# Attention scores on three PSUM banks, broadcasts and small transposes on the two banks of the attention transposes

## The chip, the cores and the metric

The kernel runs on one core of a Trainium2 chip. The metric is the device time of one execution in microseconds. The engines are called as the profile calls them: PE (TensorE, the matrix engine; PEld is its weight load), DVE (VectorE), ACT (ScalarE), POOL (GpSimd), SP (SyncE, which issues the DMAs). Matmuls write to PSUM, which has eight banks of 512 float32 values in each of 128 partitions; this kernel uses all eight.

## The reference, cut to what matters

Two layers over 1024 latent tokens and 256 context tokens, width 1024. Each layer is a mixer of three head groups on one input projection, and a gated MLP with a convolution of width 3:

```python
h = modulate(rms_norm(x, norm1_g[i]), sh1, sc1)
a_z, bq, bk, bv, cq, ck, cv = split_proj(h @ w_in[i])
out_a = chunk_gmlp(a_z, a_ws[i], a_bs[i])                               # A: gMLP over chunks of 128
out_b = window_attn_latent(q_b, k_b, v_b, k_bc, v_bc, b_sink[i])        # B: 8 heads, window +-128, context
s = jnp.einsum('bqhmd,bkhmd->bhmqk', q, k).astype(jnp.float32) * q.shape[-1] ** -0.5
p = jax.nn.softmax(s, axis=-1)                                          # C: 4 heads, two maps each,
pd = p[:, :, 0] - lam * p[:, :, 1]                                      #    all 1280 keys
o_c = jnp.einsum('bhqk,bkhd->bqhd', pd.astype(v.dtype), v)
x = x + g1 * (jnp.concatenate([out_a, out_b, out_c], axis=-1) @ w_out[i])
x = x + g2 * conv_ffn(modulate(rms_norm(x, norm2_g[i]), sh2, sc2),
                      w_up[i], conv_w[i], conv_b[i], w_down[i])         # d_ff 2816
```

The context tokens go through the same layer (not in the last one), and attend to context tokens alone.

## The kernel before, in words

The code is written straight down, and a scheduler of the build then orders each engine's instructions: an instruction that stands later in the text goes ahead of an earlier one if its inputs and its buffer are there sooner. Tiles come from pools; each name (tag) in a pool has so many buffers, which are handed out in the order of the text. So the order of the work depends on the number of buffers and on who shares them. On the chip, each engine then works its own list in order.

Large matrix products are made of three products of split operands (a high part and a rest, `TERMS`), in `mm3`: L130 with weights stationary (output projection and MLP), L132 with tokens stationary (input projection). They write to PSUM tiles `z`. In some phases, called wide, every second one goes to a bank of the scores and is called `zS`. Weights come by DMA into `raw`; ACT makes the high part of `wsp` (L115), POOL subtracts (L109), one subtraction for each 128 rows of a large block.

- `inproj` (input projection, L401): for each tile of 128 tokens 24 products L132 of 512 columns, then norms and rotary terms on DVE and POOL, then `to_scratch`, which transposes the result on PE (L379) into a tile `U`, from where ACT and DVE write it out. For group A, L455 mixes positions, also into `U`.
- `units_b` (mixer B): one unit is one of 2 kv heads for two query tiles. Scores L545, L547 to L550, L557, L558 into tiles `S`; DVE takes maxima (L473), ACT exponentials; transposes L586 into `T`, products with V L596 into `O`, a broadcast L606 into `T`.
- `units_c` (mixer C): one unit is one head for two query tiles. For each tile and map three scores L669 (512, 512 and 256 keys) into `S`, each read by DVE (L473); ACT exponentials (L672); DVE joins the maps (L679); transposes L704 into `T`; L695 (products with V) into `O`; two small transposes L722, L745 into `T`.
- `prep` (L781): output projection of a group of tokens (L130), then `norm_tile` for each 128 tokens: a transpose (L205) and a broadcast (L214) into `U`, and with them the input of the MLP. The first norms of a layer take `T` in the same way.
- `mlp` (L817): up projection and convolution, 22 blocks of two halves of 24 products each, and down projection.

In layer 0 the text has: projections and attention of the context tiles (8, 9) and tiles 0, 1, more projections, attention of tiles 2, 3, `prep` of the first token group, attention of tiles 4 to 7, and the MLP of three token groups, the latter two of them wide. In layer 1: norms and projections, C and B of tiles 0, 1 between them, attention of tiles 2 to 5 (`A1[0]`: four B units, then eight C units), `prep(1, G1[0])` (256 tokens, which needs only tiles 0 and 1), attention of tiles 6, 7, and the MLP of three groups (256, 386 and 386 columns).

The PSUM pools, and who calls them:

```python
932    psA = mkpool("psA", 1, "right", PSUM)
933    psS = mkpool("psS", 2, "right", PSUM)
934    psT = mkpool("psT", 1, "right", PSUM)
935    psD = mkpool("psD", 2, "left", PSUM)
936    mkS = lambda: psS.tile([P, 512], F32, tag="S", name="S")
937    mkT = lambda: psT.tile([P, 512], F32, tag="T", name="T", bufs=2)
938    mkU = lambda: psT.tile([P, 512], F32, tag="U", name="U")
939    mkO = lambda: psA.tile([P, 512], F32, tag="O", name="O")
942    def mkz():
944        if zc[1] and zc[0] % 2:
945            return psS.tile([P, 512], F32, tag="S", name="zS")
946        return psD.tile([P, 512], F32, tag="z", name="z")
```

So before: one bank for `O`, two for `S`, two for `T`, one for `U`, two for `z`.

Of the kernel before, what the change touches and what calls it, by code (L numbers as in the profile page):

```python
# [10 lines left out]
F32 = mybir.dt.float32  # L11
# [5 lines left out]
PSUM = bass.MemoryType.PSUM  # L17
# [15 lines left out]
P = 128  # L33
# [19 lines left out]
def trunk(ctx: ExitStack, tc: tile.TileContext, a: dict):  # L53
# [3 lines left out]
    def mkpool(name, bufs, side="left", space=None):  # L57
        kw = {"space": space} if space is not None else {}
        return tc.alloc_tile_pool(name=name, bufs=bufs, side=side, reuse_waits="tile", **kw)
# [870 lines left out]


    psA = mkpool("psA", 1, "right", PSUM)
    psS = mkpool("psS", 2, "right", PSUM)
    psT = mkpool("psT", 1, "right", PSUM)
    psD = mkpool("psD", 2, "left", PSUM)
    mkS = lambda: psS.tile([P, 512], F32, tag="S", name="S")
    mkT = lambda: psT.tile([P, 512], F32, tag="T", name="T", bufs=2)
    mkU = lambda: psT.tile([P, 512], F32, tag="U", name="U")
    mkO = lambda: psA.tile([P, 512], F32, tag="O", name="O")
    zc = [0, False]  # L940

# [279 lines left out]
```

## Time and profile before

| | |
|---|---|
| time, median of 3 runs | 3387.66 us (3386.68 to 3388.7) |
| the profiled execution's time | 3388.27 us |
| its span, first to last instruction | 3386.5 us |
| mean granted clock of PE | 0.965 |
| PE busy | 3168.0 us, 94% |
| DVE, ACT, POOL busy | 64%, 49%, 59% |

Busy time of PE counts an instruction from its start to its end, waiting operands left out; a product of 512 columns at a lower granted clock is busy for longer. Float32 products (L695, L596, L606, L455) leave two records each in the trace, the others one. Durations of one instruction overlap on PE, so the rate is read from a stretch: records over time.

### The profile page before, as it was taken

The numbers are of one execution on the slowest core, as the hardware profiler recorded it, in microseconds if no ns is written. First come the engines' busy times: TensorE is split into PE (matmuls) and PEld (weight loads), VectorE is DVE, ScalarE is ACT, GpSimd is POOL, SyncE is SP. The second block draws the span as 40 slices with busy tenths as digits, with TensorE's granted clock in tenths as the row PEclk, the third lists the DMA queues.
The fourth block names the chain that finished last, engine by engine and source line by source line (L and its number), as shares of the span: only waits on it lengthen the run. The fifth ranks groups of instructions, "written<-read, shape, count | busy, mean of one in ns | idle before, by whom it ended". The sixth has DMA issues, their size and how long they took to land. (4 is left out here: it accounts for less than half of the span.)

```text
span 3386.5 us, 56854 instructions
## 1 busy us (share of the span) xinstructions
PE 3168.0 (94%) x19695; PEld 2771.2 (82%) x19695; DVE 2178.7 (64%) x5026; ACT 1666.9 (49%) x2931; POOL 1992.6 (59%) x3233
## 2 busy tenths in 40 slices
PE   6989988899999999898999899899999999999999
PEld 4767656787898888898999777667888789999998
DVE  4776764766767973659555478757876674465455
ACT  3554545655555433533344344557665553344443
POOL 2754213444565777767566454325777566787776
PEclk7999989899999999999999999999999999999999
DMA  9555785335443664278333555445555536334443
GB/s 267 169 149 147 227 252 167 108 115 134 128 117 94 197 205 118 87 194 247 97 95 109 163 132 165 127 147 143 151 148 157 133 108 185 113 111 137 128 118 113
DMA packets 766431, 499.67 MB, mean 148 GB/s; under 512 B 81480, under 2 KB 722368, under 8 KB 766144
## 3 DMA queue, kind: packets, MB, share of 16 engines
q1 hardware_dynamic: 766144, 496.03, 51.4%
q8 instruction: 157, 2.57, 0.3%
q14 instruction: 130, 1.06, 0.1%
HBM read 432.48 MB, written 63.44 MB: 146 GB/s over the span
## 5 line engine op out<-in xcount | busy, mean ns | idle before, releaser
L109 POOL TENSOR_TENSOR wsp<-raw,wsp 128x128 fp32r<-128x128 f32 (+2 forms) x2838 | 1615.8, 606 | 800.8 <-ACT wsp L115 757.2
L130 PE MATMUL z<-h,wsp 128*128 128x386 f32 (+3 forms) x5280 | 881.4, 319 | 12.2 <-DVE t L844 6.6
L130 PEld LDWEIGHTS z<-h,wsp 128*128 128x128 f32 x5280 | 827.8, 191 | 26.4 <-issue 13.6
L115 ACT ACTIVATE wsp<-raw 128x1024 fp32r<-128x1024 f32 (+2 forms) x660 | 556.0, 846 | 486.1 <-PE z L130 169.2
L130 PE MATMUL z<-g,wsp 128*128 128x386 f32 (+3 forms) x2640 | 463.5, 324 | 29.2 <-DVE xg L869 13.9
L130 PEld LDWEIGHTS z<-g,wsp 128*128 128x128 f32 x2640 | 419.0, 192 | 45.7 <-issue 20.2
L132 PE MATMUL z<-wsp,h 128*128 128x512 f32 x1584 | 410.4, 405 | 11.2 <-ACT wsp L115 4.9
L132 PEld LDWEIGHTS z<-wsp,h 128*128 128x128 f32 x1584 | 294.9, 193 | 79.7 <-ACT wsp L115 6.2
L130 PE MATMUL zS<-h,wsp 128*128 128x386 f32 (+1 forms) x2112 | 339.0, 313 | 6.1 <-DVE t L844 5.3
L130 PEld LDWEIGHTS zS<-h,wsp 128*128 128x128 f32 x2112 | 318.8, 190 | 10.7 <-issue 3.7
L837 ACT ACTIVATE t<-z,cw 128x386 f32<-128x386 f32 (+3 forms) x220 | 137.8, 627 | 209.0 <-PE z L130 208.6
L869 DVE SCALAR_TENSOR_TENSOR xg<-z,mods,xg 128x384 f32<-128x384 f32 (+5 forms) x288 | 140.1, 501 | 145.1 <-PE z L130 144.1
L841 DVE SCALAR_TENSOR_TENSOR t<-z,cw,t 128x255 f32<-128x255 f32 (+3 forms) x264 | 132.0, 500 | 142.2 <-ACT t L837 141.8
L672 ACT ACTIVATE ec<-ec,nmc 128x1280 f32<-128x1280 f32 (+1 forms) x144 | 182.1, 1265 | 63.8 <-DVE ec L473 63.5
L130 PE MATMUL z<-oT,wsp 128*128 128x384 f32 (+2 forms) x1056 | 200.8, 337 | 5.4 <-DMA oT<-o_s 2.1
L473 DVE TENSOR_SCALAR_CACHE_REDUCE ec<-S,nmc 128x512 f32<-128x512 f32 (+1 forms) x256 | 156.5, 611 | 76.7 <-PE S L669 73.1
L130 PEld LDWEIGHTS z<-oT,wsp 128*128 128x128 f32 x1056 | 178.7, 190 | 13.8 <-issue 2.8
L130 PE MATMUL zS<-g,wsp 128*128 128x386 f32 (+1 forms) x1056 | 181.1, 314 | 6.9 <-DVE t L844 2.8
L669 PE MATMUL S<-Kc,qc 128*128 128x512 f32 (+1 forms) x400 | 157.5, 417 | 23.9 <-DVE ec L473 22.1
L851 DVE SCALAR_TENSOR_TENSOR th<-th,t 128x386 f32<-128x386 f32 (+3 forms) x132 | 143.7, 1088 | 52.9 <-ACT th L850 52.7
L360 POOL TENSOR_TENSOR rs<-ss,cst 128x8 f32<-128x8 f32 (+1 forms) x76 | 113.2, 1490 | 103.7 <-DVE ss L358 99.7
L130 PEld LDWEIGHTS zS<-g,wsp 128*128 128x128 f32 x1056 | 161.1, 189 | 12.4 <-ACT wsp L115 3.8
(247 smaller groups left out, 4682.6 us busy)
## 6 DMA issues: line engine op xcount, KB each, us to landing
raw<-in_w_up_dram SPq DMA_DIRECT2D x264, 512.0 KB
mraw<-in_w_ada_dram SPq DMA_DIRECT2D x96, 512.0 KB
raw<-in_w_down_dram SPq DMA_DIRECT2D x192, 256.0 KB
Kc<-qk_s SPq DMA_DIRECT2D x96, 320.0 KB
raw<-in_w_in_dram SPq DMA_DIRECT2D x52, 512.0 KB
raw<-in_w_out_dram SPq DMA_DIRECT2D x48, 512.0 KB
raw<-in_w_down_dram SPq DMA_DIRECT2D x104, 192.0 KB
qk_s<-st SPq DMA_DIRECT2D x18, 512.0 KB
```

The costliest lines, as they stand in the source:

```text
L109: eng.tensor_tensor(out=lo, in0=src, in1=hi.bitcast(F32), op=ALU.subtract)
L115: act.activation(out=hl[:, 0], in_=raw, func=AF.Copy)
L130: pe.matmul(ps, w(i, k), h(j, k), start=s, stop=e)
L132: pe.matmul(ps, h(i, k), w(j, k), start=s, stop=e)
L360: pool.tensor_tensor(out=rs[:, :ns], in0=ss[:, 1, :ns], in1=mhalf[:, :ns], op=ALU.pow)
L473: dve.tensor_scalar(out=neg, in0=s_ap, scalar1=-1.0, scalar2=init, op0=ALU.mult, op1=ALU.min, accum_out=acc)
L669: pe.matmul(S[:, :w_], q[:, m, ti * P:ti * P + P], K[m][:, o:o + w_], start=True, stop=True)
L672: act.activation(out=e[:, :nk], in_=e[:, :nk], func=AF.Exp, scale=-1.0, bias=acc, accum_out=l1[:, m, ti:ti + 1])
L837: act.activation(out=t[:, o:o + n], in_=ps[:, :n], func=AF.Identity, scale=cw[:, L, 1, ft:ft + 1], bias=cw[:, L, 3, ft:ft + 1])
L841: dve.scalar_tensor_tensor(out=t[:, o + b + 1:o + e], in0=ps[:, b:e - 1], scalar=cw[:, L, 0, ft:ft + 1], in1=t[:, o + b + 1:o + e], op0=AL ...
L851: dve.scalar_tensor_tensor(out=th[:, :N], in0=th[:, :N], scalar=1.0, in1=tg[:, :N], op0=ALU.add, op1=ALU.mult)
L869: dve.scalar_tensor_tensor(out=xs, in0=ps[:, b + o0:b + o1], scalar=mods[:, L, 40 + ct, s:s + 1], in1=xs, op0=ALU.mult, op1=ALU.add)
```

## The change

Two places in the text: the scores' pool has three buffers, and the tiles `U` are taken with the tag and the two buffers of `T`.

```diff
     psA = mkpool("psA", 1, "right", PSUM)
-    psS = mkpool("psS", 2, "right", PSUM)
+    psS = mkpool("psS", 3, "right", PSUM)
     psT = mkpool("psT", 1, "right", PSUM)
     psD = mkpool("psD", 2, "left", PSUM)
     mkS = lambda: psS.tile([P, 512], F32, tag="S", name="S")
     mkT = lambda: psT.tile([P, 512], F32, tag="T", name="T", bufs=2)
-    mkU = lambda: psT.tile([P, 512], F32, tag="U", name="U")
+    mkU = lambda: psT.tile([P, 512], F32, tag="T", name="U", bufs=2)
     mkO = lambda: psA.tile([P, 512], F32, tag="O", name="O")
```

The banks are then one for `O`, three for `S` (and `zS`), two for `T` and `U` together, two for `z`. The instructions are the same; the scheduler puts them in another order. Three places of the PE order show it.

First, layer 1, the norms of `prep(1, G1[0])` (L205 and L214 into `U`). Before, the first norm stands among the B units of tiles 2 to 5:

```order
L586 MATMUL T<-cst,pb 128x128 x4
L596 MATMUL O<-PT,Vb 64x256 x2
L586 MATMUL T<-cst,pb 128x128 x4
L205 MATMUL U<-cst,red 128x128
L557 MATMUL S<-Kb,qb 128x256
L558 MATMUL S<-Kb,qb 128x256
L557 MATMUL S<-Kb,qb 128x256
L558 MATMUL S<-Kb,qb 128x256
L596 MATMUL O<-PT,Vb 64x256 x2
```

With the change both norms stand behind the last small transpose (L745) of the eighth C unit of these tiles:

```order
L557 MATMUL S<-Kb,qb 128x256
L558 MATMUL S<-Kb,qb 128x256
L745 MATMUL T<-cst,o_26375 128x128
L205 MATMUL U<-cst,red 128x128
L214 MATMUL U<-dg,cst 128x128
L205 MATMUL U<-cst,red 128x128
L214 MATMUL U<-dg,cst 128x128
L586 MATMUL T<-cst,pb 128x128 x8
L596 MATMUL O<-PT,Vb 64x256 x2
```

They moved by some 650 instructions, past all C units of tiles 2 to 5, and the MLP's products, which need them, moved along.

Second, the same eight C units. Before, at the end of the first of them, the MLP's products (`h` is its input) stand between the scores:

```order
L695 MATMUL O<-PT,Vc 64x128 x3
L130 MATMUL z<-h_26706,wsp 128x256 x10
L669 MATMUL S<-Kc,qc 128x256
L722 MATMUL T<-cst,on 128x128
L669 MATMUL S<-Kc,qc 128x512
L130 MATMUL z<-h_26706,wsp 128x256 x22
L669 MATMUL S<-Kc,qc 128x512
L130 MATMUL z<-h_26706,wsp 128x256 x2
L669 MATMUL S<-Kc,qc 128x256
```

With the change, at the end of the second of them:

```order
L695 MATMUL O<-PT,Vc 64x128 x3
L669 MATMUL S<-Kc,qc 128x512
L669 MATMUL S<-Kc,qc 128x256
L722 MATMUL T<-cst,on 128x128
L669 MATMUL S<-Kc,qc 128x512 x2
L669 MATMUL S<-Kc,qc 128x256
L669 MATMUL S<-Kc,qc 128x512 x2
L669 MATMUL S<-Kc,qc 128x256
L745 MATMUL T<-cst,o_25463 128x128
L704 MATMUL T<-cst,ec 128x128 x8
L695 MATMUL O<-PT,Vc 64x128
```

The scores of the next unit follow each other with no product of the MLP between them.

Third, layer 0, the B units of the context tiles. Before, they alternate with the input projection (L132) and its transposes into `U` (L379):

```order
L586 MATMUL T<-cst,pb 128x128 x4
L379 MATMUL U<-cst,ko 128x128 x3
L132 MATMUL z<-wsp,h 128x512 x7
L586 MATMUL T<-cst,pb 128x128 x4
L596 MATMUL O<-PT,Vb 64x256 x2
L586 MATMUL T<-cst,pb 128x128 x4
L132 MATMUL z<-wsp,h 128x512 x7
L379 MATMUL U<-cst,ko 128x128 x3
L132 MATMUL z<-wsp,h 128x512 x8
L596 MATMUL O<-PT,Vb 64x256 x2
```

With the change they begin behind the last C unit of the context and stand alone:

```order
L557 MATMUL S<-Kb,qb 128x256
L558 MATMUL S<-Kb,qb 128x256
L722 MATMUL T<-cst,on 128x128
L745 MATMUL T<-cst,o_2043 128x128
L586 MATMUL T<-cst,pb 128x128 x8
L596 MATMUL O<-PT,Vb 64x256 x2
L586 MATMUL T<-cst,pb 128x128 x4
L596 MATMUL O<-PT,Vb 64x256 x2
```

The input projection of the other tiles, with its transposes, follows behind them.

## The prediction

> **What bounds the kernel now.** I read the head of the page, then busy time in chosen stretches, then the waits, then groups by shape.
>
> The page says how full each engine is:
>
> ```profile
> span 3386.5 us, 56854 instructions
> PE 3168.0 (94%) x19695; PEld 2771.2 (82%) x19695; DVE 2178.7 (64%) x5026; ACT 1666.9 (49%) x2931; POOL 1992.6 (59%) x3233
> ```
>
> PE is the bound on average: 218 us of the span are left in which it does nothing. Busy is not the same as fast, though, so I looked at stretches. The PE order gives the places: where at least 15 PE instructions stand in a row with none of the large products (L130, L132) among them, and how much attention is in each such run. These are the eight longest of the kernel before after the start (columns: stretch, its length, busy time and number of records of PE, PEld, DVE, ACT, POOL, granted clock, DMA):
>
> ```profile
> 206.00:219.00 13.00, 6.92 (x29) 4.61 (x28) 12.65 (x56) 7.38 (x24) 5.71 (x5) 0.73 0.71 226
> 334.00:386.00 52.00, 48.00 (x358) 26.91 (x356) 36.31 (x121) 26.53 (x57) 14.05 (x14) 0.93 0.91 268
> 429.00:481.00 52.00, 41.20 (x298) 24.93 (x295) 35.81 (x121) 24.02 (x44) 7.50 (x12) 0.78 0.98 276
> 495.00:526.00 31.00, 21.43 (x139) 14.78 (x138) 11.98 (x58) 14.11 (x33) 1.44 (x2) 0.83 0.84 253
> 582.00:622.00 40.00, 25.23 (x102) 15.01 (x102) 34.79 (x87) 31.95 (x60) 12.99 (x16) 0.69 0.56 149
> 2194.00:2232.00 38.00, 32.76 (x198) 21.60 (x198) 19.63 (x85) 17.19 (x38) 3.28 (x3) 0.85 0.57 175
> 2235.00:2257.00 22.00, 20.59 (x141) 12.57 (x140) 11.56 (x52) 12.87 (x28) 1.29 (x1) 1.00 0.45 126
> 2303.00:2338.00 35.00, 29.70 (x177) 18.14 (x175) 26.36 (x83) 24.69 (x49) 10.70 (x18) 0.85 0.55 141
> ```
>
> Against them two stretches where attention and large products alternate on PE:
>
> ```profile
> 640.00:760.00 120.00, 119.62 (x764) 105.79 (x762) 80.31 (x241) 66.22 (x121) 69.47 (x125) 1.00 0.40 115
> 2380.00:2740.00 360.00, 337.35 (x2508) 294.33 (x2508) 260.19 (x678) 224.06 (x406) 244.24 (x414) 0.97 0.55 148
> ```
>
> The reader is to see that attention with cover keeps PE at 119.6 of 120 us and the clock at 1.00, while attention without cover leaves PE 57 us idle in 283 us, at clocks down to 0.69, and that in 206:219 and 582:622, where mixer C stands alone, DVE is the full engine (12.65 of 13, 34.79 of 40). So the kernel lives on mixing attention with large products, and what decides the time is how much attention stands alone.
>
> **The change, part by part.** No instruction is added or taken away; durations stay. What follows from the two edited lines is this.
>
> *The order.* The names T and U now draw on one set of two banks, and a set hands its banks out in the order of the program text. In the built order of 677 tiles named T or U, before the change a tile stands 81 times directly ahead of one that the text has earlier, and with it never. So a small transpose of the input projection (L379, L455) or a broadcast of `prep`'s norm (L205, L214) that stands behind an attention block in the text can't be made until every transpose of that block is made. In layer 1 the norms of `prep(1, G1[0])` move behind all of the attention of tiles 2 to 5, and the gated MLP, which would have covered it, waits for them. In layer 0 the same happens to the input projections and to `prep(0, G0[0])`. Counted in the PE order, in the long runs: mixer C without cover is 213 instructions before, 982 after, at 54 a unit (12 scores, 22 transposes, 20 products with V) that is 4 units and 18; mixer B without cover is 627 and 1070, at about 110 a unit some 6 units and 10. One run in layer 1 alone has 878 instructions: eight C units and four B units without a large product.
>
> *The price of a C unit alone.* The products with V (L695) leave two records each, so a unit is 74 records. Covered, at 119.62 us for 764 records, that is 0.157 us a record, 11.6 us. Alone, DVE sets it (columns: count, busy us, mean ns of one, idle before it and what ended that; the fifth row has shortest, median and longest):
>
> ```profile
> L679 DVE SCALAR_TENSOR_TENSOR ec<-ec,rho 128x1280 f32<-128x1280 f32 x64 | 106.5, 1664 | 1.2
> L473 DVE TENSOR_SCALAR_CACHE_REDUCE ec<-S,nmc 128x512 f32<-128x512 f32 x128 | 95.3, 745 | 26.5 <-PE S L669 24.6
> L473 DVE TENSOR_SCALAR_CACHE_REDUCE ec<-S 128x512 f32<-128x512 f32 x128 | 87.6, 684 | 39.1 <-PE S L669 19.0 <-PE T L704 16.9 <-PE T L586 2.8
> L473 DVE TENSOR_SCALAR_CACHE_REDUCE ec<-S,nmc 128x256 f32<-128x256 f32 x128 | 61.2, 478 | 50.1 <-PE S L669 48.5
> L473 DVE DVE_READ_ACCUMULATOR ec<-S,nmc x256: 73/82/101, 382.1 to 2774.0; 128x1 f32 x128
> L677 DVE SCALAR_TENSOR_TENSOR rho<-l,nlam,rho 128x1 f32<-128x1 f32 x72 | 23.6, 328 | 1.6
> ```
>
> Four rounds of three maxima, 0.684 + 0.745 + 0.478 and three reads of 0.082, make 8.6 us; two combinations of 1.664 make 3.3; the small scalars (0.328 twice here, and some ten of that kind, taken at 0.3) make about 3.7: 15.6 us of DVE a unit. DVE reached 34.79 of 40 us in 582:622, so I take 15.6 / 0.87 = 18 us. A unit that loses its cover costs 18 - 11.6 = 6.4 us, and 14 of them 90 us. The bounds: 15.6 - 11.6 = 4.0 each (56 us) if DVE never waits; 0.40 us a record as in 206:219 and 582:622 together (53 us, 131 records), 30 us a unit and 18 each (258 us), but those two stretches also hold norms and projections on DVE, so I stay near the lower one.
>
> *The price of a B unit alone.* In the three stretches from 2194 to 2338 B makes 516 records in 95 us, 0.184 each against 0.157; at some 130 records (the products with V and the broadcasts count double) a unit loses 3.5 us, and 4 more units lose 14 us (0 to 20, the last by 0.198 of the slowest of the three).
>
> *What is left without attention.* Attention that ran alone no longer dilutes the MLP. Behind the last attention of layer 1 the order now has 640 products 256 columns wide; before, it has none there. They need weights faster than POOL splits them:
>
> ```profile
> L130 PE MATMUL z<-h,wsp 128*128 128x256 f32 x1054 | 138.5, 282 | 1.8 <-DVE xg L869 1.6
> L109 POOL TENSOR_TENSOR wsp<-raw,wsp 128x128 fp32r<-128x128 f32 x140 | 62.5, 490 | 12.8 <-ACT wsp L115 12.8
> ```
>
> The first row is 2340 to 2800 us, the second 2840 to 2935 us, where the MLP runs alone. One block of `w_up` is 24 products, 24 x 138.5 / 1054 = 3.2 us of PE, and eight subtractions, 8 x 0.490 = 3.9 us of POOL. About two thirds of the 640 are of `w_up`, 18 blocks at 0.8 us: 14 us (0 to 25). The wider blocks of later groups have PE above POOL and don't change.
>
> *Relief.* Stretches that mixed attention with the MLP were not free: PE misses 22.7 of 360 us in 2380:2740. About half of that attention is gone from there: 11 us, with some 4 us in layer 0, together 15 us gained (0 to 25).
>
> *The third score bank, and five in turn for wide phases.* PE's wait for a score bank and DVE's for a score are these (us in total, times, longest):
>
> ```profile
> PE S L669 <- DVE ec L473: 22.1, 27, 2.1
> DVE ec L473 <- PE S L669: 92.6, 86, 4.3
> ```
>
> With DVE as the bound a third bank lets PE run one score ahead and then wait again, so I count nothing on PE; that DVE finds its scores ready is in the 0.87. In the wide phases (two MLPs of layer 0, the last of layer 1) the order is the same but for a few rows; the large products that alternate there still have two of their own banks: nothing. What hides it is that those products stand at PE's rate already.
>
> Sum: +90 + 14 + 14 - 15 = +103 us on the profiled execution's 3388.3 us (3386.5 of span and 1.8 around it; the median of the runs is 3387.7, 0.6 less, which I neglect): 3388.3 + 103 = 3491 us.
>
> **The rivals.**
> *PE becomes the slow engine in the uncovered runs.* Point: when the granted clock in them falls so far that a C unit's 11.6 us of PE exceeds DVE's 18, that is below 0.64. Two stretches of 20 us are below it:
>
> ```profile
> 40.00:60.00 20.00, 11.90 (x43) 8.83 (x44) 14.80 (x32) 12.46 (x22) 8.42 (x7) 0.54 0.90 239
> 600.00:620.00 20.00, 10.07 (x29) 5.01 (x28) 15.93 (x44) 14.98 (x32) 5.68 (x4) 0.61 0.40 95
> ```
>
> At 0.54 a unit is 11.6 / 0.54 = 21.5 us: 14 x 9.9 = 139, and with 20 for B, 14 and -15, +158: 3546 us. For it: 0.69, 0.73, 0.78 in C's longer stretches. Against it: 2235:2257 stays at 1.00. The Trainium skill, in TensorE: Matmul & The Clock Gate (Part 1), says that PE's clock falls to half after an idle window of about 3.4 us and comes back after as long a busy one; by that rule, with all of these units at half clock, one takes 23 us and the time would be about 3569 us. The trace agrees that the clock falls where PE idles (0.69 in 582:622, 1.00 in 640:760), but shows no long stretch at half.
> *The uncovered units cost little.* DVE is fed by three banks and never waits: 56 us for C, B 0, MLP 0, relief 25: +31, 3419 us. For it: DVE 12.65 of 13 in 206:219. Against it: 31 us with B and C in 495:526 had DVE at 11.98 only.
> *Faster: the third bank feeds DVE and the order costs nothing.* Place: the chains of L473. It would take away PE's 22.1 us and give 3388 - 22 = 3366 us. It decides if a C unit alone needs no more than the 11.6 us of a covered one; DVE's rows add to 15.6, which speaks against it. The Trainium skill's Perfetto Trace Analysis (Optimizing Tensor Performance, Matmuls) has matmul groups rotate through different banks so that reading one overlaps filling the next, which is this rival; DVE's 92.6 us of waiting for scores agrees that there is something to overlap.
> *No change.* It would need the 1070 and 982 uncovered instructions to be covered by something else, or the gains to meet the losses: relief of 25 and 22 against 56 at least.
>
> **How the numbers follow.** Forecast (C alone by DVE, slower by 45 to 165 us): 0.74. PE slow (3535 and above): 0.12. Cheap (3400 to 3430): 0.08. Faster: 0.04. No change: 0.02. A measurement tells about 0.2% (7 us) from no change. The time is the forecast's, 3491. The range leaves out the faster cases, the lower half of the cheap one and most of PE slow: 3420 to 3570. Slower: 0.74 + 0.12 + 0.08 = 0.94.
>
> **What would show it.** In the profile after, the long run of layer 1 (eight C and four B units, no L130) lasts 200 to 240 us, with DVE near 0.8 and a clock of 0.7 to 0.9, and PE's wait for L473 grows from 22.1 us to over 60. Mean clock falls below 0.965 and PE's idle time grows by 60 us or more; DVE's busy total stays near 2179. The stretch of 256-wide products behind it shows PE waiting for wsp. The two MLPs of layer 0's second and third group last as before. I am wrong if the long run goes at PE's rate (about 150 us), or if the large products stand between the units after all.

## The result, and the profile after

The changed kernel takes 3653.9 us (median of four runs, 3643.9 to 3661.7) against 3387.9 for the kernel before on the same chip: ratio 1.078, 95% interval 1.0761 to 1.0799. It is 266 us slower; the forecast was 103 us slower. One run each of e4 and e15 below ran at a far lower granted clock (5006.1 us at 0.555, 4485.1 us at 0.636), and what is given for these two is their other three runs.

The head of the page after:

```profile
span 3649.0 us, 56873 instructions
PE 3279.3 (90%) x19695; PEld 2823.1 (77%) x19695; DVE 2223.7 (61%) x5026; ACT 1680.7 (46%) x2931; POOL 1964.6 (54%) x3233
```

The same 19695 products on PE, but PE is idle for 370 us of the span instead of 218, and its busy time grew by 111 us although no product was added: the mean granted clock went from 0.965 to 0.931. So of the 263 us by which the span grew, 152 are idle time of PE and 111 are busy time.

The order shows in where the large products (L130, L132) pause. Before, the trace has seven pauses of over 15 us, together 273 us (the longest 52.6). After it has eight, together 698 us. Their windows in the trace after (stretch, length, busy time and records of PE, PEld, DVE, ACT, POOL, granted clock, DMA):

```profile
215.00:235.00 20.00, 9.56 (x32) 5.25 (x31) 17.43 (x68) 12.73 (x36) 6.80 (x8) 0.58 0.56 157
239.00:325.00 86.00, 68.47 (x391) 42.28 (x389) 42.22 (x213) 46.46 (x121) 6.70 (x7) 0.82 0.29 77
422.00:518.00 96.00, 68.79 (x476) 43.39 (x475) 60.97 (x194) 42.73 (x85) 15.20 (x15) 0.79 0.63 181
550.00:593.00 43.00, 32.79 (x214) 17.17 (x213) 12.89 (x43) 8.70 (x15) 8.38 (x19) 0.61 0.86 256
657.00:756.00 99.00, 65.92 (x378) 44.21 (x377) 58.82 (x184) 55.80 (x112) 16.25 (x22) 0.71 0.37 101
2199.00:2253.00 54.00, 38.27 (x220) 25.37 (x218) 28.70 (x96) 25.57 (x51) 3.07 (x5) 0.74 0.26 71
2298.00:2341.00 43.00, 40.22 (x250) 24.72 (x248) 23.81 (x113) 24.58 (x55) 3.55 (x3) 0.92 0.24 68
2409.00:2664.00 255.00, 198.26 (x1129) 124.95 (x1130) 158.51 (x537) 138.37 (x269) 22.78 (x33) 0.80 0.36 97
```

The reader is to see three things. The forecast's long run of layer 1 is there (2409 to 2664). Half of the time in pauses (344 of 696 us) lies in layer 0, before 760 us, where the prediction had little. And only in the first (DVE, 17 of 20 us) and the seventh (PE, 40 of 43 us) is an engine nearly full. POOL has almost nothing to do there, because it is the large products that need POOL, and none of them is in turn.

PE's waits after, and three of the kernel before that the prediction did not show (us in total, times, longest):

```profile
PE S L669 <- DVE ec L473: 40.2, 39, 2.8
PE z L130 <- DVE t L844: 35.8, 20, 8.5
PE T L745 <- DVE o L741: 26.2, 12, 3.7
PE U L214 <- DVE dg L212: 18.7, 9, 6.5
PE U L205 <- DVE red L203: 16.6, 6, 7.4
PE z L130 <- ACT wsp L115: 12.3, 11, 4.3
```

```profile
PE z L130 <- DVE t L844: 12.5, 12, 2.8
PE U L214 <- DVE dg L212: 12.4, 4, 7.6
PE T L745 <- DVE o L741: 8.5, 5, 3.5
```

No single wait carries it: short links of the attention's own chain (L473, L741) and of the norm's (L203, L212) grew, as they would with nothing else there for PE to do meanwhile. The wait for L844 is in the MLP; it comes back with e9 and in the last section.

To put the loss in place I cut both traces into slices of 10 us, and gave each PE instruction the distance to the next start that it has where PE is fed without a pause at full clock (a least-squares fit over stretches of 40 records of the trace before, so an estimate: 0.178 us for a product of 386 columns, 0.249 for a score of 512, 0.121 for a transpose L704). Slice length less that work is what the slice lost:

| slices, by their main work | time, before to after | PE's work | lost |
|---|---|---|---|
| mixer C (large products under 30%) | 100 to 310 us | 50 to 169 | 50 to 141 (+91) |
| mixer B (the same) | 180 to 330 | 138 to 228 | 42 to 102 (+60) |
| modulation (L144, L149) | 60 to 100 | 31 to 50 | 29 to 50 (+21) |
| norms, small transposes, start | 20 to 40 | 4 to 8 | 16 to 32 (+16) |
| large products 30 to 90% | 1520 to 1010 | 1405 to 882 | 115 to 128 (+13) |
| large products over 90% | 1510 to 1860 | 1411 to 1701 | 99 to 159 (+59) |

The sum is +260 us, nearly the whole difference of the spans (262.5). That is no test, since PE's work is the same in both: the table says where the time went, as an estimate, to some 5 us a line.

### The profile page after: what moved, and what is told of

Its sections match the earlier page's. It is cut to its first block, busy times and chain, and to the rows that moved or that the text cites. A ratio compares the mean times of both kernels' runs of the same rounds, so it can differ in the third digit from the quotient of the medians.

```text
span 3649.0 us, 56873 instructions
## 1 busy us (share of the span) xinstructions
PE 3279.3 (90%) x19695; PEld 2823.1 (77%) x19695; DVE 2223.7 (61%) x5026; ACT 1680.7 (46%) x2931; POOL 1964.6 (54%) x3233
## 5 line engine op out<-in xcount | busy, mean ns | idle before, releaser
L109 POOL TENSOR_TENSOR wsp<-raw,wsp 128x128 fp32r<-128x128 f32 (+2 forms) x2838 | 1598.7, 600 | 738.4 <-ACT wsp L115 696.0
L130 PE MATMUL z<-h,wsp 128*128 128x386 f32 (+3 forms) x5280 | 889.0, 322 | 41.4 <-DVE t L844 26.3
L130 PEld LDWEIGHTS z<-h,wsp 128*128 128x128 f32 x5280 | 833.5, 193 | 63.9 <-issue 34.4
L115 ACT ACTIVATE wsp<-raw 128x1024 fp32r<-128x1024 f32 (+2 forms) x660 | 557.2, 847 | 588.0 <-PE z L130 183.4
L130 PE MATMUL z<-g,wsp 128*128 128x386 f32 (+3 forms) x2640 | 460.2, 323 | 27.5 <-DVE xg L869 10.4
L130 PEld LDWEIGHTS z<-g,wsp 128*128 128x128 f32 x2640 | 418.0, 192 | 44.4 <-issue 12.8
L132 PE MATMUL z<-wsp,h 128*128 128x512 f32 x1584 | 407.1, 407 | 9.5 <-ACT wsp L115 4.5
L132 PEld LDWEIGHTS z<-wsp,h 128*128 128x128 f32 x1584 | 299.3, 195 | 78.5 <-ACT wsp L115 5.6
L130 PE MATMUL zS<-h,wsp 128*128 128x386 f32 (+1 forms) x2112 | 340.0, 313 | 2.4 <-POOL wsp L109 1.2
L130 PEld LDWEIGHTS zS<-h,wsp 128*128 128x128 f32 x2112 | 317.6, 189 | 9.5 <-POOL wsp L109 7.7
L851 DVE SCALAR_TENSOR_TENSOR th<-th,t 128x386 f32<-128x386 f32 (+3 forms) x132 | 179.9, 1363 | 65.5 <-ACT th L850 65.1
L738 POOL TENSOR_TENSOR crs<-css,cst 128x2 f32<-128x2 f32 x36 | 27.0, 751 | 327.9 <-DVE css L735 326.8
L130 PE MATMUL z<-oT,wsp 128*128 128x384 f32 (+2 forms) x1056 | 194.8, 339 | 4.6 <-DMA oT<-o_s 4.5
L130 PE MATMUL zS<-g,wsp 128*128 128x386 f32 (+1 forms) x1056 | 182.1, 314 | 10.4 <-POOL wsp L109 3.9
L130 PEld LDWEIGHTS z<-oT,wsp 128*128 128x128 f32 x1056 | 178.2, 192 | 12.4 <-issue 6.6
L130 PEld LDWEIGHTS zS<-g,wsp 128*128 128x128 f32 x1056 | 161.1, 190 | 16.4 <-POOL wsp L109 6.5
L473 DVE TENSOR_SCALAR_CACHE_REDUCE ec<-S,nmc 128x512 f32<-128x512 f32 (+1 forms) x256 | 156.8, 614 | 22.4 <-PE S L669 12.7
```

Source lines behind the costliest of these rows:

```text
L109: eng.tensor_tensor(out=lo, in0=src, in1=hi.bitcast(F32), op=ALU.subtract)
L115: act.activation(out=hl[:, 0], in_=raw, func=AF.Copy)
L130: pe.matmul(ps, w(i, k), h(j, k), start=s, stop=e)
L132: pe.matmul(ps, h(i, k), w(j, k), start=s, stop=e)
L473: dve.tensor_scalar(out=neg, in0=s_ap, scalar1=-1.0, scalar2=init, op0=ALU.mult, op1=ALU.min, accum_out=acc)
L851: dve.scalar_tensor_tensor(out=th[:, :N], in0=th[:, :N], scalar=1.0, in1=tg[:, :N], op0=ALU.add, op1=ALU.mult)
```

## Is it the order, the missing bank, or the third bank?

The theory throughout is the prediction's: one set of banks is handed out in text order, so small transposes wait behind attention, and attention stands without large products. The rivals are that the loss comes from having a bank fewer for T and U, or from the third score bank.

**e1: the shared set gets three banks, the scores two** (the edit is to the kernel before). Nothing is lost in number; only the sharing remains.

```diff
-    mkT = lambda: psT.tile([P, 512], F32, tag="T", name="T", bufs=2)
-    mkU = lambda: psT.tile([P, 512], F32, tag="U", name="U")
+    mkT = lambda: psT.tile([P, 512], F32, tag="T", name="T", bufs=3)
+    mkU = lambda: psT.tile([P, 512], F32, tag="T", name="U", bufs=3)
```

> Two score banks as before, and T and U share one set of three banks, so the small tiles have as many banks as before and only the order in which they are handed out is tied to the text. If the order is the cause (attention left without large products beside it, as in the 878 instructions of layer 1, which this kernel's PE order has again with 880): the time of the changed kernel, 3620 to 3690 us. If the lost bank is the cause (two banks for T and U in place of three): the time of before, 3380 to 3400 us. If the third score bank is the cause: the time of before as well.

Measured 3612.6, ratio 1.0675 (1.0643 to 1.0708): +228 us, just below the theory's range and far from the rival's. Sharing alone is most of the loss.

**e7: after, with two score banks; the eighth bank stays unused.**

```diff
-    psS = mkpool("psS", 3, "right", PSUM)
+    psS = mkpool("psS", 2, "right", PSUM)
```

> After's shared set of two banks for T and U, but two score banks as before, so that one bank of PSUM is left unused. What differs from after is the third score bank alone. Theory (the order does it, the third bank hardly counts): within 15 us of after, 3640 to 3670. Rival (the third bank helps DVE a little and hid part of the loss): 3675 to 3710. Rival (with three score banks the scores run ahead and push large products back, so the third bank is part of the loss): 3590 to 3635. Since three shared banks with two for scores gave 3613, a result near 3654 would also say that the 41 us between those two are the price of the bank taken from the transposes and broadcasts.

Measured 3644.1, ratio 1.0779 (1.0739 to 1.0818): not to be told from after. So beside the shared set the third score bank is worth nothing that can be told (the interval is some 26 us wide), as the prediction counted it, and the 31 us between e1 and e7 (35 by the ratios) are the price of the bank that T and U lost together.

**e2: three score banks, T and U kept apart with one bank each** (the edit is to the kernel after).

```diff
-    mkT = lambda: psT.tile([P, 512], F32, tag="T", name="T", bufs=2)
-    mkU = lambda: psT.tile([P, 512], F32, tag="T", name="U", bufs=2)
+    mkT = lambda: psT.tile([P, 512], F32, tag="T", name="T", bufs=1)
+    mkU = lambda: psT.tile([P, 512], F32, tag="U", name="U")
```

> Three score banks as in the change, T and U one bank each with names of their own: the same eight banks, the third score bank kept, the sharing undone. If the shared order is the cause: close to before, 3390 to 3450 us, a little slower because T has one bank and its PE order has 948 B and 792 C instructions in runs without a large product against 823 and 588 before. If the third score bank is the cause: 3600 us or more.

Measured 3581.5, ratio 1.058 (1.055 to 1.061): a miss. The variant was not clean: with one bank for the attention's transposes PE waits for that bank (in its trace, the third line; after has no such line in its longest waits):

```profile
PE S L669 <- DVE ec L473: 52.1, 43, 6.5
PE z L144 <- DMA mraw<-in_w_ada_dram: 21.8, 20, 3.2
PE T L586 <- ACT PT L590: 20.2, 18, 4.3
```

It also leaves attention alone again: the large products pause for 126 us from 1111 us on, in the attention of layer 0, where neither before nor after has a pause. So it says nothing on the third bank; e7 does. What it does say is that a bank taken from T, beside a third for the scores and without any sharing, costs 197 us, nearly as much as sharing without a lost bank; the two losses don't add up in after, where the lost bank is worth 31 us.

**e5 and e6: before's banks, with one user of U moved to T.** In e5 the norms of `prep` (L205, L214), in e6 the input projection's transposes (L379, L455).

```diff
e5  -  norm_tile(L, 1, ..., mkU, big, ...)      e6  -  inproj(..., mkz, mkU, w)
    +  norm_tile(L, 1, ..., mkT, big, ...)          +  inproj(..., mkz, mkT, w)
```

> The banks of before; only the norms of prep take their tiles from T in place of U. One part of the shared order alone: the PE order has the long run of layer 1 again (674 instructions, all eight C units of tiles 2 to 5), and layer 0's run of C and B ahead of the norms (292), but the input projections as before. Order theory, from what the changed kernel lost against PE's work in those stretches (layer 1 from 2405 to 3010 us of its trace, some 100 us more than before; layer 0 from 660 to 760 us, some 20 more): 3480 to 3540 us. If the projections carry the loss: under 3420 us.

> The banks of before; only the input projections (inproj) take their tiles from T in place of U. The other part alone: attention of the context and of tiles 0 and 1 stands without large products, as in the change, while prep's norms go ahead as before. Order theory: the rest of the change's loss, 3490 to 3550 us, so that this and the one with prep's norms alone add up to about +266 us. If prep's norms carry the loss: under 3430 us.

Measured 3522.2 (1.0404, 1.0375 to 1.0433) and 3511.8 (1.0374, 1.0343 to 1.0404): +138 and +128, both as expected. Their sum is 266, the change's whole loss; that it meets it so exactly is partly chance, since each is known to about 10 us. Each user brings its half by standing behind the attention, with all eight banks in use as before.

**e8: before's banks, T and U shared in layer 0 only.**

```diff
-    mkU = lambda: psT.tile([P, 512], F32, tag="U", name="U")
+    ul = ["T", 2]
+    mkU = lambda: psT.tile([P, 512], F32, tag=ul[0], name="U", bufs=ul[1])
...
+    ul[:] = ["U", 1]
     M = mkpool("M1", 2, "left")
```

> Before's banks; T and U share two banks only until layer 0's third MLP, and have banks of their own from there on. Theory (layer 0 lost what the two traces show between their milestones, 1417 against 1527 us for the last attention of layer 0): +100 to +125, 3485 to 3515. The prediction's own sum had only 20 to 25 us of its 103 in layer 0, that is 3405 to 3415. Rival (what layer 0 loses early it gets back later, since the MLPs behind it have less attention between their products): 3420 to 3460.

Measured 3529.9, ratio 1.0428 (1.04 to 1.0455): +144 us, above the theory's range and six times what the prediction had there. The marks agree: the products L183 stand in the wide MLPs of layer 0, and their first and last starts are, before, after and in e8:

```profile
L183 PE MATMUL U<-modr,four x16: 196/206/217, 1417.1 to 1738.4; 128*32 128x32 f32 x16
L183 PE MATMUL U<-modr,four x16: 196/229/263, 1527.1 to 1847.5; 128*32 128x32 f32 x16
L183 PE MATMUL U<-modr,four x16: 196/207/218, 1538.3 to 1867.7; 128*32 128x32 f32 x16
```

After is 110 us late at the first one already. From the first to the last it takes 320.4 us against 321.3: the wide MLPs around them did not change. Sliced as in the table up to there (1420 us before, 1530 after), layer 0 lost 114 us more: by this estimate 34 in mixer B, 28 where attention and large products mix, 38 in modulation and norms, and only 9 in mixer C.

**e3 and e4: the text moved, `prep` ahead of attention that it doesn't need**, with after's banks and with before's.

```diff
-    attn(0, [(2, 3)])
     x1 = prep(0, G0[0], X1, M)
+    attn(0, [(2, 3)])
...
+    x1 = prep(1, G1[0], X1, M)
     for t in A1[0]:
         attn_b(1, t, at, mkS, mkT, mkO)
     for hd in range(4):
         attn_c(1, hd, A1[0], at, mkS, mkT, mkO)
-    x1 = prep(1, G1[0], X1, M)
```

> After's banks; in the program text prep(0, G0[0]) stands ahead of the attention of tiles 2 and 3, and prep(1, G1[0]) ahead of the attention loops of A1[0]. Then a set that hands out banks in text order gives the norms theirs before that attention. In the built PE order the run of 878 instructions without a large product is gone; in all, C without cover falls from 1054 to 783 instructions (5 units) and B from 1365 to 1181 (1.7 units). Theory (order; a C unit costs some 8 us more alone than covered, a B unit some 5 to 10, and the norms no longer stand behind the attention with nothing beside them): 50 to 100 us less than after, 3555 to 3605. Rival (the long run was not what cost; banks or the clock are): 3640 to 3660.

> Before's banks with the same two moves in the text. There the sets of T and U already let the norms go first, so the theory of order expects little: B without cover goes from 823 to 1037 instructions, C from 588 to 579: 3385 to 3425. Rival (the text's place of prep costs something in before as well): 3340 to 3375. It is also the trial whether the moved text makes a kernel faster than both.

e3: 3624.5, ratio 1.0712 (1.0683 to 1.0742), by the ratios some 23 us less than after, where 50 to 100 were expected: a miss. The long run is gone, but by the slices of e3's trace C is still 260 us the main work, and the pauses have moved: mixer C of layer 0 now stands alone up to some 1250 us, with the next group's norms behind it. With this order of the text, too, something stands behind the attention. e4: 3414.3 (1.0093, 1.0067 to 1.0119), slower by 28 us, as expected; so this is no better kernel.

## What do the units cost, alone and covered?

**e12 and e13: mixer C done twice in the kernel before**, eight units where nothing covers them, and four in layer 1, three of them between large products.

```diff
e12      attn(0, [(4, 5), (6, 7)])
     +   for hd in range(4):
     +       attn_c(0, hd, [(4, 5), (6, 7)], at, mkS, mkT, mkO)
e13      for hd in range(4):
             attn_c(1, hd, A1[1], at, mkS, mkT, mkO)
     +   for hd in range(4):
     +       attn_c(1, hd, A1[1], at, mkS, mkT, mkO)
```

> The kernel before with mixer C of tiles 4 to 7 in layer 0 done twice (eight units more; the same values are written again). The built PE order has 427 more instructions in a run without large products: the eight units stand alone. The forecast's price of a unit alone, 18 us: +144, 3520 to 3545. If an uncovered unit went at a covered unit's 11.6 us: +93, 3475 to 3490. If also the norms behind it wait: up to 20 more, 3545 to 3565.

> The kernel before with mixer C of tiles 6 and 7 in layer 1 done twice (four units more, the same values written again). In the built PE order all but 47 to 64 of their 216 instructions stand between large products: three units covered and one alone. The prediction's price of a covered unit, 11.6 us: 3 x 11.6 + 18 = +53, 3435 to 3445. If a covered unit takes 9 us of PE only, since the 0.157 us a record came from a stretch that holds large products too: 3 x 9 + 18 = +45, 3427 to 3436. If the attention hides behind waits of the MLP for its weights (POOL): +20 to +35, 3408 to 3424. So the covered price is best read from the growth of PE's work, and this run says whether it is nearer 12 or below 9.

e12: 3560.7, ratio 1.0523 (1.0503 to 1.0543), +175 us, 22 a unit. The time lies in the branch in which the norms behind them wait too; that this is why is not shown. e13: 3447.7, ratio 1.0187 (1.0167 to 1.0206), +62 us, a little above all branches and nearest to the prediction's price: less 22 for the one alone, 13 for a covered unit. So losing its cover costs a C unit 9 us by these two, and 6 by the slices (91 us over some 14 units, at 8.7 us of PE's own work a unit); forecast 6.4.

**e14 and e15: mixer B done again in the kernel before**, four units alone, and four mostly covered.

```diff
e14      attn(0, [(4, 5), (6, 7)])
     +   for t in ((4, 5), (6, 7)):
     +       attn_b(0, t, at, mkS, mkT, mkO)
e15  -   for t in A1[1]:
     +   for t in A1[1] + A1[1] + A1[1]:
             attn_b(1, t, at, mkS, mkT, mkO)
```

> The kernel before with mixer B of tiles 4 to 7 in layer 0 done a second time behind everything else of that attention (four units; the same values are written again). In the built PE order 399 more instructions stand in a run without large products: the four units are alone. The prediction's price of a B unit alone, 130 records at 0.184: 24 us each, +96, 3475 to 3490. By the slices of the two traces (330 - 180 us more for 93 us more of B's own PE work, 17 us a unit): 28 us each, +112, 3490 to 3510. If B alone is slower still, by its loads of keys or its one bank for products with V: above 3520.

> The kernel before with mixer B of tiles 6 and 7 in layer 1 done three times (four units more, the same values written again). In the built PE order 142 of their 392 instructions fall into short runs of 15 or more without large products, none into a long one: the units are mostly covered. The prediction's price of a covered unit, 130 records at 0.157: 20.4 us, +82, 3460 to 3475. By 17.4 us of PE work, the sum of start-to-start distances where PE is never idle: +70, 3450 to 3462. Then the loss of cover is worth 28 - 17 = 10 us a unit instead of 3.5.

e14: 3504.0, ratio 1.0344 (1.0318 to 1.037), +113 us by the medians, 28 a unit, as the slices had it. e15: 3442.8, ratio 1.0159 (1.013 to 1.0189), +52 us by the medians, 13 a unit, below both branches: covered B costs less than PE's own work for it (17.4 us by the fit), so part of it seems to go into pauses of the MLP. By these two runs a B unit that loses its cover costs 15 us; forecast 3.5. The stretches without a large product in e14 (B) and e12 (C):

```profile
1124.00:1232.00 108.00, 81.13 (x482) 51.44 (x482) 91.89 (x283) 48.96 (x107) 9.23 (x12) 0.81 0.40 117
1129.00:1294.00 165.00, 113.98 (x582) 72.40 (x580) 141.82 (x371) 76.55 (x141) 11.62 (x16) 0.71 0.35 95
```

DVE is busy for 0.85 and 0.86 of them, but for a good part not with attention. The modulation of layer 1 (L168 to L175), which this attention of layer 0 doesn't need, runs on DVE in both; its largest row in each (B, then C):

```profile
L170 DVE SCALAR_TENSOR_TENSOR mev<-mraw,cpad,mev 128x512 f32<-128x512 f32 x52 | 37.6, 752 | 1.6 <-DMA mraw<-in_w_ada_dram 1.6
L170 DVE SCALAR_TENSOR_TENSOR mev<-mraw,cpad,mev 128x512 f32<-128x512 f32 x53 | 38.6, 751 | 0.0
```

With L168, L174 and L175 it makes 51.4 of DVE's 91.89 us and 52.4 of its 141.82. What is left fills 0.37 and 0.54 of the stretches. So neither run shows that attention alone fills DVE, and the prices of 28 and 22 us may hold some waiting behind this work.

**e10 and e11: is it DVE that sets a C unit alone?** The combination L679 is cut to 128 columns, in after and in before: the rest of the second softmax is left out.

```diff
-  dve.scalar_tensor_tensor(out=es[0][:, :nk], in0=es[1][:, :nk], ..., in1=es[0][:, :nk], ...)
+  dve.scalar_tensor_tensor(out=es[0][:, :128], in0=es[1][:, :128], ..., in1=es[0][:, :128], ...)
```

> After, with the combination of the two softmaxes (L679) done for 128 columns instead of all 768 or 1280: the rest of the second softmax is left out of the result. It takes about 2.9 us of DVE from each C unit (two of 1.66 us become two of about 0.2). Theory (a C unit alone goes at the pace of its chain through DVE): in after about 17 units' worth of time is spent on C alone (310 us in 10-us slices of the trace in which C is the main work), so 17 x 2.9 = 50 us less: 3590 to 3620. Rival (PE at a lowered clock sets the pace, DVE does not): within 15 us of after, 3640 to 3660.

> The same shortened combination in the kernel before, as the control: about 100 us are spent on C alone there, 5 to 6 units: 15 us less by the theory, 3365 to 3380; then the distance between the two kernels shrinks from 266 to some 230 us. Rival: unchanged within 8 us, and the distance stays at 266.

e10: 3641.6, 1.0763 (1.0735 to 1.0792), by the ratios 6 us less than after, not to be told from no change. That is the range of the rival, by which PE at a lowered clock sets the pace. e11: 3356.7, 0.9922 (0.9898 to 0.9945), 29 us less than before. The distance did not shrink, it is 285 us: a miss. In the eight units of the long run the work taken off DVE came back about half. The starts of L722, one a unit, and the windows between them, in after and in e10:

```profile
L722 PE MATMUL T<-cst,on x8: 270/272/328, 2513.8 to 2641.1; 128*128 128x128 f32 x8
2514.00:2641.00 127.00, 97.92 (x548) 64.57 (x547) 87.33 (x288) 68.01 (x133) 4.88 (x7) 0.76 0.23 59
```

```profile
L722 PE MATMUL T<-cst,on x8: 270/272/328, 2519.0 to 2637.5; 128*128 128x128 f32 x8
2519.00:2637.00 118.00, 94.61 (x548) 62.72 (x547) 71.32 (x284) 67.37 (x131) 4.88 (x7) 0.81 0.24 63
```

Seven intervals: 127.3 / 7 = 18.2 us a unit, then 118.5 / 7 = 16.9. DVE loses 16 us of work, the stretch 9, and no engine is full in either. The first and the last interval are not whole units, so here are the four units between the second and the sixth start, in after, in e10, and in e7, which has two score banks and DVE's whole work:

```profile
2529.70:2605.90 76.20, 57.55 (x299) 36.35 (x299) 51.95 (x159) 39.87 (x74) 2.79 (x4) 0.73 0.25 63
2537.20:2604.90 67.70, 53.94 (x298) 34.79 (x296) 40.91 (x153) 38.32 (x72) 2.78 (x4) 0.80 0.26 68
2537.40:2604.50 67.10, 53.57 (x297) 34.05 (x295) 50.65 (x154) 38.77 (x73) 2.78 (x4) 0.80 0.27 69
```

That is 19.0, 16.9 and 16.8 us a unit, with 13.0, 10.2 and 12.7 us of DVE in it. e7 goes as fast as e10 though its DVE has 2.4 us more to do, and in after a unit alone is longer than in e7 by 2.2 us, with nothing but the third score bank between them (one profiled execution each). So the pace forecast (18) is nearly right, and its reason (DVE at 0.87) is not: DVE is at 0.68 in after. It is a chain through DVE, ACT and PE, with PE at 0.73 to 0.80 of its clock. Which of its links counts most, and how much of it is the clock, was not settled.

## The stretch of 256-wide products

**e9: after, every fourth subtraction of the weight split on DVE** in layer 1's first MLP group.

```diff
-                sub(eng, hl[:, 1, k], raw[:, k], hl[:, 0, k])
+                sub(dve if st.get("alt") and k % 4 == 3 else eng, hl[:, 1, k], raw[:, k], hl[:, 0, k])
...
+    st["alt"] = 1
     mlp(1, G1[0], *x1, M, hook)
+    st["alt"] = 0
```

> After, with every fourth subtraction of the weight split (L109, 128 columns) in layer 1's first MLP group done by DVE instead of POOL. Theory (the 153 us of 256-wide products behind the attention lose about 47 us, and POOL, busy 115.6 us of 153 there, sets them): a quarter less on POOL makes 3.9 us a block 2.9, under PE's 3.2: 15 to 40 us less than after, 3610 to 3640. Rival (the loss there is ACT's copy of the weights, the DMA or DVE's convolution, not POOL): within 8 us of after. Rival (DVE's subtraction queues behind the attention's chains and delays weights): 10 to 30 us more.

Measured 3629.6, ratio 1.0708 (1.0682 to 1.0734): about 24 us less than after, inside the theory's range. The stretch between the last attention and the next group's output, in after and in e9:

```profile
2858.00:3007.00 149.00, 122.66 (x790) 117.16 (x789) 72.02 (x115) 59.64 (x93) 113.23 (x222) 0.89 0.49 145
2848.00:2986.00 138.00, 120.60 (x820) 115.00 (x819) 85.09 (x170) 62.87 (x100) 99.19 (x177) 0.95 0.54 160
```

POOL's work falls by 14 us, the stretch by 11, with 30 more records of products in it. PE's two longest waits in these stretches, in after and in e9:

```profile
PE z L130 <- DVE t L844: 13.0, 4, 8.5
PE z L130 <- ACT wsp L115: 7.1, 4, 4.3
```

```profile
PE z L130 <- ACT wsp L115: 4.1, 3, 1.6
PE z L130 <- DVE t L844: 3.6, 5, 1.8
```

PE waits 3.0 us less for weights, and 9.4 us less for DVE. Of these, 8.5 are one operation of DVE that stood still for 10 us while POOL subtracted (last section); in e9's stretch no such operation (L851) takes over 1.1 us. So it is shown that less work on POOL shortens this stretch. That POOL sets it by splitting the weights too slowly, as forecast, is not shown: most of the gain is a stall of DVE that went away. The stretch also begins 10 us sooner, which was not followed up.

## Why the prediction was wrong in its size

The mechanism of the order was right: e1, e5 and e6 show that order costs the time, e7 that the third bank brings nothing. The direction holds. The sum (+103), the range (to 3570) and the likeliest case (slower by 45 to 165 us) do not; by its time alone the result lies under "PE slow (3535 and above)", which had 0.12. By the slices the sum missed 46 us for B, 73 for the MLP and the relief, and 37 for what was not in it.

- **C alone (forecast +90): the sum came out, in good part by luck.** The slices give +91, and the loss of cover 6 to 9 us a unit for 6.4. But the price was 15.6 us of DVE at 0.87, and four units of the long run have 13.0 us at 0.68: two errors that cancel, 18 for 19.0. The 0.87 was read in 582:622, where some 11 of DVE's 34.79 us are a norm's (L203, L207, L212, L216). PE's wait for L473 rose to 40 us, not over 60, and the long run lasted 255 us for 200 to 240.
- **B alone (+14): the step that failed first.** The slices give +60. The price was a mean per record in three stretches of B against the mean of a stretch mixed with large products: 0.184 less 0.157. But a record of B is on average shorter than one of a large product (by the fit, 0.130 us for a transpose L586, 0.178 for a product of 386 columns), so that mean charged covered B with the large products' time: 20.4 us, where the fit has 17.4 and e15 has 13. And alone it takes 28 (e14, with the modulation on DVE beside it), not 24.
- **MLP without attention and relief (+14 - 15): failed, the first in its reason too.** The slices give +59 and, for mixed ones, +13. The prediction took a subtraction on POOL at its mean duration, 0.490 us, but these records overlap: the busy time in the row that it shows is 62.5 us for 140, and the train of 32 in the last section takes 13.36 us. That is 0.45 and 0.42 each, so a block takes POOL 3.3 to 3.6 us, little more than PE's 3.2. Over the whole kernel the waits of L130 for weights (L115, L109) grew by 6 us, from 17.5 to 23.1, and those for L844 by 15, from 20.6 to 35.8. With them grew L851, the operation that stands ahead of L844 on DVE (before, then after):

```profile
L851 DVE SCALAR_TENSOR_TENSOR th<-th,t 128x386 f32<-128x386 f32 (+3 forms) x132 | 143.7, 1088 | 52.9 <-ACT th L850 52.7
L851 DVE SCALAR_TENSOR_TENSOR th<-th,t 128x386 f32<-128x386 f32 (+3 forms) x132 | 179.9, 1363 | 65.5 <-ACT th L850 65.1
```

  That is also most of why DVE's total did not stay near 2179 us but rose to 2223.7. These waits make 21 of the 59 us at most; the rest is open. The relief did not come: attention and MLP, mixed, lost 115 us in 1520 before and lose 128 in 1010 after.
- **Not in the sum: +37.** Modulation (L144) stands in slices of its own for 100 us instead of 60: the pauses 422 to 518 and 550 to 593 above have the highest DMA shares of all, 0.63 and 0.86. And the norm chains of `prep` behind the last attention unit have nothing beside them. In layer 0 and in layer 1:

```profile
720.00:756.00 36.00, 14.89 (x54) 9.05 (x54) 12.05 (x27) 18.52 (x40) 9.37 (x7) 0.54 0.23 72
2641.00:2664.00 23.00, 11.56 (x43) 7.37 (x44) 10.34 (x32) 10.08 (x22) 5.71 (x5) 0.59 0.42 120
```

  The text said "in layer 0 the same happens" and then priced units only. In the long runs of the two traces layer 0 has 198 instructions of C more (203 and 401), 3.7 units or some 23 us at the forecast's 6.4; e8 shows 144.
- **PE slow by clock: not as that rival had it, but not excluded.** A unit alone took 19.0 us at a clock of 0.73, not 21.5 at 0.54. But 111 of the 263 us are busy time of PE at a lower mean clock, and e10 came out where the clock's rival had it. How much of the loss a full clock would have spared was not measured.
- **What held:** the mean clock fell, PE's idle time grew by 152 us (60 or more), the wide MLPs of layer 0 stayed, and the long run went nowhere near PE's rate.

## What to carry to other kernels

In a build like this one, a PSUM tag that two stages share is an ordering rule: the later stage waits for the last bank of the earlier one, and what is lost is all that could have run beside it; before merging tags, list what stands behind each user in the text. To price such a loss, take alone and covered costs per unit of each kind of work, by doing that unit twice in both places, never as a mean per instruction over a mixed stretch; and look at what else has moved into the stretch before calling an engine full. And count every serial chain (norms, modulation) that the new order leaves with nothing beside it, in each stage.

## What was not expected of the hardware

One DVE operation (L851, two float32 inputs in SBUF; shortest 0.42 us, median 0.70) took 10.06 us in the 256-wide stretch, and PE waited 8.54 us for the L844 queued behind it. The timeline after (start, length, engine, line, tiles, count, idle before):

```profile
2907.91 13.36 POOL L109 TENSOR_TENSOR wsp<-raw,wsp 128x128 fp32r<-128x128 f32 x32
2911.48 10.06 DVE L851 SCALAR_TENSOR_TENSOR th<-th,t 128x256 f32<-128x256 f32 x1 [0.55 <-ACT th L850]
2921.97 0.48 DVE L844 SCALAR_TENSOR_TENSOR t<-z,cw,t 128x255 f32<-128x255 f32 x1
2922.60 1.62 PE L130 MATMUL z<-h,wsp 128*128 128x256 f32 x6 [8.54 <-DVE t L844]
...
3085.78 8.01 POOL L109 TENSOR_TENSOR wsp<-raw,wsp 128x128 fp32r<-128x128 f32 x19
3086.91 7.30 DVE L851 SCALAR_TENSOR_TENSOR th<-th,t 128x386 f32<-128x386 f32 x1 [0.65 <-ACT th L850]
3094.77 0.62 DVE L844 SCALAR_TENSOR_TENSOR t<-z,cw,t 128x385 f32<-128x385 f32 x1
```

Both times DVE's operation ends some 0.3 to 0.4 us after POOL's train of back-to-back subtractions (2921.27 and 3093.79). Fifteen such stalls of over 2.5 us stand in the trace after, ten in that before, and all of them end 0.3 to 0.6 us after the last subtraction of such a train. The Trainium skill, SBUF — State Buffer (SBUF: two separate sides), says that a DVE operation with two SBUF inputs and a POOL operation that reads SBUF lock a shared port against each other for the length of an instruction. The trace agrees that DVE is held up, but until the end of the train, some 23 and 16 subtractions further, and not for one of about 0.42 us. That it is this lock was not tested by a run of its own.
